# A hybrid attention and GLA decoder step: GLA's steps at thirds of a tile, and products in pairs over two PSUM banks

## Chip, core and metric

The kernel runs on one core of one Trainium2 chip. The metric is the device time of one execution in microseconds (us); the median of three runs of the kernel before is 1816.8 us (1815.72 to 1818.68). A difference of under 0.2% is taken as no change.

## What is computed

One layer of a decoder on 2048 prompt tokens and 8 x 8 sample tokens (2112 rows in all, 1024 channels). An input projection feeds two branches: windowed attention with sinks and a relative bias, and GLA, a linear attention with a decaying state. Both are gated, projected, merged, projected again by `w_o`, and normalized. Cut to what the change touches:

```python
z = jnp.einsum('btd,dn->btn', x, w_in)          # q k v g_att gq gk gv g_gla g_lr r_att r_gla
log_a = jax.nn.log_sigmoid(g_lr @ w_gk_up + b_gk) / 16
# GLA, per head and chunk; b is the running sum of log_a in the chunk
qt, kt, kend = qc * exp(b), kc * exp(-b), kc * exp(b_last - b)
o = qt @ S + where(causal, qt @ kt.T, 0) @ vc
S = exp(b_last) * S + kend.T @ vc
o_gla = o * rsqrt(mean(o * o, -1) + EPS) * gla_norm_w
h_att = (o_att * silu(g_att)) @ w_pa
h_gla = (o_gla * silu(g_gla)) @ w_pg
merged = sigmoid(r_att) * h_att + sigmoid(r_gla) * h_gla
x = layer_norm(DN_ALPHA * x + merged @ w_o, ln_g, ln_b)
```

## The kernel before

**Products.** Nearly all of TensorE's (PE's) time goes into float32r products of a 128 x 128 piece of weights with 352 columns of x. A factor is split into a high and a low part, so that each 128-row step takes three products: high x high, high weights x low x, low weights x high x (lines 1297 to 1299). A *group* is one product of blocks: 4 steps, 12 matmuls (6 in the sets a0 to a2), summed in one PSUM bank. The list `groups` holds 719 of them in program order, in nine sets: x0, x1, a0, u0, x2, a1, u1, a2, u2. The x sets (input projection and the two merge gates) use Strassen's scheme with seven products, numbered 1, 7, 6, 4, 5, 2, 3 in order of issue, and two column blocks (j = 0, 1) run side by side: product 1 of j = 0, product 1 of j = 1, product 7 of j = 0, and so on. Both take the same x and different weights. The four banks pd_74 to pd_77 serve in turn: products 1, 6, 5, 3 of one j share a bank, 7, 4, 2 another. The a and u sets (`w_pa`, `w_pg`) use eight plain block products; there two neighbours have the same weights and different x.

**The loop over groups** does the following for each `g`: it starts the weight loads of group g+9 (`w_first`) and of kept weights for g+5, splits the weights of group g+4 (`w_make`: POOL adds blocks at line 339, ACT casts at line 142, DVE subtracts at line 143; six buffers `wp`), issues the 12 matmuls, calls `combine`, which takes the result out of its bank (ACT copies at lines 375 and 379 for products 1, 7, 6; DVE adds at 384, 390, 396 for 4, 5, 2; a sink such as ACT's line 186, 199 or 211 for product 3), and then lets side work run: `xdo` makes the next set's x, and `tick` runs what `at(t, ...)` put down for this tick. A tick is four steps, about one group. PE follows this order exactly; the other engines' instructions are ordered by a scheduler.

**Side work on PE** is plain float32 and uses a pool `pa` of four more banks, handed out in turn. For GLA each head has tiles of 128 tokens, `st` ticks apart (5.0, 5.8 and 6.3 in the three GLA phases). A tile has four steps:
- v (`gla_v`, lines 1052 and 1053): three transposes; ACT's line 1054 copies them out (`gv`).
- a (`gla_a`, line 1062): scores; DVE's line 1064 masks them out (`aper`).
- b (`gla_b`, lines 1084, 1086, 1087): output and state, two banks, called op and sp here. DVE's line 1092 takes sp into the state `S`; ACT's 1071, POOL's 1072 and 1073 and ACT's 1074 take op through the norm (`on`).
- c (`gla_c`, line 1101): transposes of `on`; DVE's line 1103 multiplies them into `sg`.

With u the tile's number, v and a stand at u, b at u + 3/2, c at u + 3. So one tick holds c (of tile u-3), v and a together, and the tick half a tile later holds b. Each tile takes five banks of the four: c, v, a, op, sp; so sp gets the bank that c had half a tile earlier, and a the bank that op had.

**Gates.** `gate` (lines 699 to 719) takes four banks at once for one half of a set: four matmuls (704), eight activations out of them (708, 709), four Exp (713), four Ln (715, under another activation table), four DVE steps and stores. It runs twice per x set.

Of the kernel before, what the change touches and what calls it, by code (L numbers as in the profile page):

```python
# [15 lines left out]
AF = mybir.ActivationFunctionType  # L16
ALU = mybir.AluOpType
# [4 lines left out]
P = 128  # L22
# [4 lines left out]
NS = NB * TS  # L27
# [9 lines left out]
GH = 4  # L37
# [20 lines left out]
def kernel(ctx, tc, io):  # L58
    nc = tc.nc
    mm = nc.tensor.matmul  # L60
# [35 lines left out]
    def mt(tag, n, bufs, dt=F32, name=None):  # L96
        return M["p"].tile([P, n], dt, tag=tag, name=name or tag, bufs=bufs)
# [26 lines left out]
    def at(t, fn):  # L124
        side.setdefault(max(int(t), now[0]), []).append(fn)
# [383 lines left out]
    ops = {}  # L509
# [16 lines left out]
    def lowrank(o):  # L526

        s = o.s
        ps = pa()
        for k in range(4):  # L530
            for j in range(4):
                r = slice(32 * j, 32 * j + 32)
                mm(ps[r, :T], wg[:, k + 4 * (j // 2), :], o.r[j // 2, j % 2][:, k * T:(k + 1) * T], start=(k == 0),
                   stop=(k == 3), tile_position=(0, 32 * j))
        g_ = mtile("fin", name="glh")
        nc.scalar.copy(g_, ps[:, :T])
        for j in range(4):
            r0 = 16 * (j // 2)
            nc.gpsimd.dma_start(gl_d[r0:r0 + 16, toks(s, j % 2)], g_[32 * j:32 * j + 16])
# [39 lines left out]
        o0.mix(r0[0, 1], r0[0, 1], r0[0, 0], ALU.subtract)  # L579
        o0.make(5, r0[0, 1])  # L580

    for g, f in ((4, lambda: o0.make(3, r0[1, 1])), (6, c7), (10, c6), (12, c4), (14, lambda: lowrank(o0)), (14, c5)):
# [116 lines left out]
    def gate(B):  # L699
        ts = toks(B["s"], B["t"])  # L700
        ps = [pa() for _ in range(GH)]
        for h in range(GH):
            r = slice(32 * h, 32 * h + 32)
            mm(ps[h][:, :T], wgk[r], B["x"][r], start=True, stop=True, tile_position=(32 * h, 0))
        zs, ms = [], []
        for h in range(GH):
            z, m = mtile("fin", name="zg"), mt("lg", T, 4, name="mg")
            nc.scalar.activation(z, ps[h][:, :T], AF.Abs, bias=bgk[:, h:h + 1])
            nc.scalar.activation(m, ps[h][:, :T], AF.Relu, scale=-1.0, bias=nbgk[:, h:h + 1])
            zs.append(z)  # L710
            ms.append(m)
        for z in zs:
            nc.scalar.activation(z, z, AF.Exp, scale=-1.0)
        for z in zs:
            nc.scalar.activation(z, z, AF.Ln, bias=1.0)
        for h in range(GH):
            nc.vector.scalar_tensor_tensor(ms[h], ms[h], -1.0, zs[h], ALU.mult, ALU.subtract)
            nc.sync.dma_start(zg_d[h][:, ts], ms[h])
            wrote(zg_d[h], 0, ts)

    AS = {}
# [433 lines left out]
    def gla_phase(s, t0, t1):  # L1155
        at(t0, lambda: mpool(f"cg{s}"))
        at(t0, rings)
        nu = sum(-(-T_ // P) for _, T_ in GCH[s]) * GH
        b0 = t0 + 14
        st = (t1 - b0 - 3) / (nu + 2)  # L1160
        u = 0
        for h, (c0, T_) in ([(h, c) for c in GCH[s] for h in range(GH)] if s == 1 else
                            [(h, c) for h in range(GH) for c in GCH[s]]):
            if True:
                last = c0 + T_ == NT
                Tp = T_ - (NS if last else 0)
                nt = Tp // P
                B = dict(h=h, t0=c0, T=T_, Tp=Tp, nt=nt, last=last)
                tt = lambda v: b0 + st * v + 0.01
                b = tt(u)  # L1170
                at(b - 13, lambda B=B: gla_load(B))
                at(b - 10, lambda B=B: gla_load_v(B))
                at(b - 8, lambda B=B: gla_z(B))
                at(b - 3, lambda B=B: gla_kq(B))
                for i in range(nt):
                    at(tt(u + i), lambda B=B, i=i: gla_v(B, i))
                    at(tt(u + i), lambda B=B, i=i: gla_a(B, i))
                    at(tt(u + i + 3 / 2), lambda B=B, i=i: gla_b(B, i))
                    at(tt(u + i + 3), lambda B=B, i=i: gla_c(B, i, P, i * P))
                at(tt(u + 1) + 3, lambda B=B: gla_load_g(B))  # L1180
                o = tt(u + nt)
                u += nt
                if last:
                    u += 1
# [4 lines left out]
                    at(o + 6, lambda B=B: samp_b(B, 0))  # L1189
                    at(o + 8, lambda B=B: samp_b(B, 2))  # L1190
                    at(o + 11, lambda B=B: gla_c(B, "s", NS, B["Tp"]))
                    at(o + 12, lambda B=B: gla_store(B))
                else:
                    at(tt(u + 2) + 1, lambda B=B: gla_store(B))

    for s in range(MS):
        lo_ = {}
        for t in range(2):
            B = dict(s=s, t=t)
            g0 = base[XS[s]] + (17 if s == 0 else 2)  # L1200
            at(g0 + 4 * t, lambda B=B: gate_load(B))
            at(g0 + 5 + 4 * t, lambda B=B: gate(B))
    e = att_phase(0, 32)
    for s in range(MS):
        t1 = base[XS[s + 1]] + 30 if s < MS - 1 else base[U2] - 3
# [61 lines left out]
    half = 0  # L1267
    nm, nq = 8, 0
    NG = len(groups)
    for g, (n, q, i, s, p, b, ch) in enumerate(groups):  # L1270
        if 8 <= g + LR < NG:
            w_first(g + LR)
        if g + LK < NG:
            w_kept(g + LK)
        while nm < NG and nm <= g + (LM + 1 if groups[nm][3] == 0 and seq[groups[nm][0]] == "x0" else LM):
            w_make(nm)
            nm += 1
        for f in late.pop(g, ()):
            with tc.issue_after(pin["r"].ins):
                f()  # L1280
        while nq < NG and nq <= g + (LP + 4 if groups[nq][1] is PA_ else LP):
            _, q_, i_, s_, p_, _, _ = groups[nq]
            parts[nq] = q_.partners(i_, p_, s_)
            nq += 1
        xh, xl = ops[n].op[i[1:] if type(i) is tuple else i]
        w = wps.pop(g)
        m = q.kh * P
        if g == 8:
            banks2 = [pa() for _ in range(4)]
        ps = (banks[b] if b < 4 else banks2[b - 4])[:, :T]  # L1290
        if n == U2 and g >= start_of[U2] + 16:
            ps = banks2[b][:, :T]
        for k in range(q.kh):
            ks, ts = slice(k * P, (k + 1) * P), slice(k * T, (k + 1) * T)
            first = k == 0 and not (ch and i in (6, 4, 5, 3)) and not (type(i) is tuple and i[1])
            wh, wl = w[:, ks], w[:, m + k * P:m + (k + 1) * P]
            mm(ps, wh, xh[:, ts], start=first, stop=False, skip_group_check=ch)  # L1297
            mm(ps, wh, xl[:, ts], start=False, stop=False, skip_group_check=ch)  # L1298
            mm(ps, wl, xh[:, ts], start=False, stop=(k == q.kh - 1 and not (type(i) is tuple and i[1] == 0)), skip_group_check=ch)  # L1299
        combine(g, ps)  # L1300
        for f in xdo.get(g, ()):
            f()
        half += q.kh
        while half >= 4:
            half -= 4
            tick()
        if n == U2:
            d = g - start_of[U2]
            if d == 15:
                banks2 = [pa() for _ in range(4)]  # L1310
            if d in (4, 8, 12, 16):
                wo.append(wo_load(len(wo)))
            if d >= 28 and len(wo) < 7:
                wo.append(wo_load(len(wo)))
            if d == 3:
                ox = M["p"]
                xf, x, xr0 = load_m(1, 0, TM), [], []
            if d >= 5 and xf:
                x += [part(xf.pop(0))]
    assert not any(side.values()), [k for k in side if side[k]]  # L1320
    right.close()
    sb = right.enter_context(tc.tile_pool(name="ob", bufs=1, side="right", reuse_waits="tile"))
# [232 lines left out]
```

## Time and profile before

| | |
|---|---|
| median of three runs | 1816.8 us |
| profiled execution: its own time | 1816.59 us |
| its span, first to last instruction | 1814.8 us |
| PE, weight loads, DVE, ACT, POOL busy | 97%, 91%, 58%, 46%, 18% |
| mean granted clock | 0.994 |
| DMA | 452 MB, 249 GB/s |
| sets x0, x1, a0, u0 start at | 4.5, 446.8, 861.7, 900.4 us |
| sets x2, a1, u1, a2, u2 start at | 974.4, 1399.7, 1439.8, 1522.9, 1560.5 us |

In the timeline a row gives start, length, engine, line, what is written from what, and in brackets the idle time of the engine ahead of it with what ended it. Matmul rows overlap, so the distance of two starts, not the length, is what a matmul costs. In the view of waits a row reads: who waited, for whom, us in total, how often, the longest. In the view of windows each engine has its busy time and (x) its instructions, then PE's granted clock.

### The profile page before, as it was taken

Reading aid. Unit: us, or ns where it says so; the run is one execution under the profiler, and the core shown is the slowest. Engines: PE = TensorE matmul, PEld = TensorE weight load, DVE = VectorE, ACT = ScalarE, POOL = GpSimd, SP = SyncE. Lnnn points to the kernel's source line nnn. Section 1 sums busy time; section 2 is a strip of 40 time slices with the busy share of each in tenths; the row PEclk is TensorE's granted clock in tenths of the full one; section 3 lists DMA queues with packets and bytes.
Section 4 is the critical chain, followed back from the end, with each engine's and each line's share of the span. In section 5 each row is a group of like instructions: output and inputs, shape, how many; then the busy total and the mean of one; then the engine's idle time right before and its main releaser. Section 6 shows DMA issues by size and latency. Waiting matters only on the chain.

```text
span 1814.8 us, 31047 instructions
## 1 busy us (share of the span) xinstructions
PE 1768.1 (97%) x10850; PEld 1654.2 (91%) x10850; DVE 1059.9 (58%) x2077; ACT 837.0 (46%) x1983; POOL 334.0 (18%) x473
## 2 busy tenths in 40 slices
PE   8999999998999999999999999999999999999997
PEld 7898998998998899999999998899999889998886
DVE  7577677667546654445666456554455744536665
ACT  5856555555836553545435646444445422310100
POOL 5334344644100000000033000000000022021111
PEclk9999999999999999999999999999999999999999
DMA  6799588887698779878976897688879977975531
GB/s 211 253 313 322 208 315 283 306 274 238 223 302 275 227 244 302 275 251 276 318 217 145 276 306 223 219 293 299 284 266 320 301 197 200 325 174 175 171 102 53
DMA packets 291052, 452.03 MB, mean 249 GB/s; under 512 B 29693, under 2 KB 210229, under 8 KB 290880
## 3 DMA queue, kind: packets, MB, share of 16 engines
q1 hardware_dynamic: 263536, 416.27, 69.3%
q10 hardware_dynamic: 19536, 24.47, 3.8%
q0 software_dynamic: 7824, 9.31, 3.6%
q8 instruction: 86, 1.41, 0.3%
q14 instruction: 70, 0.57, 0.1%
HBM read 297.52 MB, written 153.30 MB: 248 GB/s over the span
## 4 chain that ended last, share of the span: by engine, by line
PE 71%; DMA 11%; ACT 4%; DVE 4%; issue 4%; POOL 3%; SPq 1%; ACTq 0%; DVEq 0%; POOLq 0%
PE pd L1297 17%; PE pd L1299 16%; PE pd L1298 16%; PE pd L1361 3%; PE pd L1360 3%; PE pd L1362 3%; POOL ws L339 2%; DMA part<-ra_d 2%; DMA ws<-w_g 1%; DMA r<-ug_d 1%; PE pa L812 1%; DMA mg_d<-fin 1%; PE pa L798 1%; PE pa L1086 1%; PE pa L766 1%
## 5 line engine op out<-in xcount | busy, mean ns | idle before, releaser
L143 DVE TENSOR_TENSOR wp<-ws,wp 128x512 fp32r<-128x512 f32 (+1 forms) x396 | 270.1, 687 | 214.6 <-ACT wp L142 195.5
L142 ACT CAST wp<-ws 128x512 fp32r<-128x512 f32 (+1 forms) x396 | 232.8, 594 | 202.0 <-PE pd L1299 137.8
L339 POOL TENSOR_TENSOR ws<-ws 128x256 f32<-128x256 f32 x162 | 141.5, 908 | 157.0 <-DVE wp L143 93.7
L1072 POOL TENSOR_SCALAR sq<-sq 128x1 f32<-128x1 f32 x68 | 21.4, 314 | 731.9 <-ACT on L1071 731.9
L375 ACT COPY m<-pd 128x352 f32<-128x352 f32 x146 | 65.4, 452 | 84.8 <-PE pd L1299 83.6
L1297 PE MATMUL pd<-x7h,wp 128*128 128x352 f32 x292 | 98.0, 336 | 5.2 <-ACT fin L186 4.3
L1361 PE MATMUL pd<-woh,x 128*128 128x512 f32 x256 | 100.0, 391 | 0.0
L1360 PE MATMUL pd<-woh,x 128*128 128x512 f32 x256 | 99.8, 390 | 0.0
L1362 PE MATMUL pd<-wol,x 128*128 128x512 f32 x256 | 99.5, 389 | 0.0
L1297 PE MATMUL pd<-x2h,wp 128*128 128x352 f32 x292 | 97.9, 335 | 0.0
L1297 PE MATMUL pd<-x3h,wp 128*128 128x352 f32 x292 | 97.8, 335 | 0.0
L1297 PE MATMUL pd<-x1h,wp 128*128 128x352 f32 x292 | 97.1, 333 | 0.7 <-ACT fin L186 0.7
L1297 PE MATMUL pd<-x6h,wp 128*128 128x352 f32 x292 | 97.3, 333 | 0.0
L1297 PE MATMUL pd<-x4h,wp 128*128 128x352 f32 x292 | 96.9, 332 | 0.0
L1297 PE MATMUL pd<-x5h,wp 128*128 128x352 f32 x292 | 96.3, 330 | 0.0
L1299 PE MATMUL pd<-x7h,wp 128*128 128x352 f32 x292 | 94.8, 325 | 1.1 <-DVE wp L143 1.1
L1299 PE MATMUL pd<-x5h,wp 128*128 128x352 f32 x292 | 94.9, 325 | 0.0
L1298 PE MATMUL pd<-x5l,wp 128*128 128x352 f32 x292 | 94.8, 325 | 0.0
L1298 PE MATMUL pd<-x1l,wp 128*128 128x352 f32 x292 | 94.8, 325 | 0.0
L1299 PE MATMUL pd<-x1h,wp 128*128 128x352 f32 x292 | 94.8, 325 | 0.0
L1299 PE MATMUL pd<-x3h,wp 128*128 128x352 f32 x292 | 94.8, 325 | 0.0
L1298 PE MATMUL pd<-x3l,wp 128*128 128x352 f32 x292 | 94.7, 324 | 0.0
(441 smaller groups left out, 5252.4 us busy)
## 6 DMA issues: line engine op xcount, KB each, us to landing
wp<-wk_w_g SPq DMA_DIRECT2D x96, 512.0 KB
ws<-w_g SPq DMA_DIRECT2D x120, 256.0 KB
wk_w_g<-wp SPq DMA_DIRECT2D x48, 512.0 KB
wp<-wk_w_ra SPq DMA_DIRECT2D x32, 512.0 KB
wp<-wk_w_rg SPq DMA_DIRECT2D x32, 512.0 KB
ws<-w_at SPq DMA_DIRECT2D x54, 256.0 KB
wp<-wk_w_at SPq DMA_DIRECT2D x24, 512.0 KB
ws<-w_pg SPq DMA_DIRECT2D x48, 256.0 KB
```

Of the source, the lines that this page charges most:

```text
L142: pin["a"] = nc.scalar.copy(dst_h, src)
L143: i = eng.tensor_tensor(dst_l, src, dst_h.bitcast(F32), ALU.subtract)
L339: nc.gpsimd.tensor_tensor(o[:, c], x[:, c], y[:, c], op)
L375: nc.scalar.copy(A[i], ps)
L766: mm(ps[kv][:, j, k0:], A["zq"][r, g0 + j, :], A["kk"][r, 0, k0:], start=True, stop=True, tile_position=(kv * HD, 0))
L1072: nc.gpsimd.tensor_scalar(sq[:n], sq[:n], EPS, None, op0=ALU.add)
L1297: mm(ps, wh, xh[:, ts], start=first, stop=False, skip_group_check=ch)
L1298: mm(ps, wh, xl[:, ts], start=False, stop=False, skip_group_check=ch)
L1299: mm(ps, wl, xh[:, ts], start=False, stop=(k == q.kh - 1 and not (type(i) is tuple and i[1] == 0)), skip_group_check=ch)
L1360: mm(ps, xh[:, xs], hi, start=(k == 0), stop=False)
L1361: mm(ps, xl[:, xs], hi, start=False, stop=False)
L1362: mm(ps, xh[:, xs], lo, start=False, stop=(k == KT - 1))
```

## The change

Three things change, and no instruction is added or removed but a few activation table loads.

1. GLA's steps: v and a stay at u, b moves to u + 5/3, c to u + 10/3. A tile's distance is now `(t1 - b0 - 3) / (nu + 7/3)`, some 1.5% less. The sample tile's steps and the store of a head move with them.
2. The gate runs in two halves of two banks, one tick apart (in x1 and x2), with the Exp and Ln part two ticks after the second half; the second gate of x1 and x2 comes 7 ticks after the first and not 4. The low-rank product of x0 moves behind group 15.
3. Groups run in pairs. If the next group has the same x (or the same weights, in the a and u sets) and another bank, both are issued together, matmul by matmul in turn; side work of the first group's tick runs in the middle of the pair, after the first half of its steps; `combine` of both follows behind the pair, then the second tick's side work. 349 pairs and 21 single groups come out. Weight making for the second group of a pair is still called for after the pair before.

```diff
-                    at(tt(u + i + 3 / 2), lambda B=B, i=i: gla_b(B, i))
-                    at(tt(u + i + 3), lambda B=B, i=i: gla_c(B, i, P, i * P))
+                    at(tt(u + i + 5 / 3), lambda B=B, i=i: gla_b(B, i))
+                    at(tt(u + i + 10 / 3), lambda B=B, i=i: gla_c(B, i, P, i * P))
...
+            at(g0, lambda B=B: gate(B, 0))
+            at(g0 + (s > 0), lambda B=B: gate(B, 2))
+            at(g0 + 3 * (s > 0), lambda B=B: gate_end(B))
...
+    def together(g):
+        if g + 1 == NG:
+            return False
+        (n, q, i, s, p, b, ch), (n_, q_, i_, s_, p_, b_, ch_) = groups[g:g + 2]
+        if n != n_ or b == b_ or type(i) is not type(i_):
+            return False
+        if i == i_:
+            return (q, p) != (q_, p_)
+        return type(i) is tuple and i[:2] == i_[:2] and (q, p) == (q_, p_)
...
+        for k in range(half * h, half * h + h):
+            ks, kl, ts = slice(k * P, (k + 1) * P), slice(m + k * P, m + (k + 1) * P), slice(k * T, (k + 1) * T)
+            for ps, w, (xh, xl) in a:
+                mm(ps, w[:, ks], xh[:, ts], start=open_ and k == 0, stop=False, skip_group_check=ch)
+            for ps, w, (xh, xl) in a:
+                mm(ps, w[:, ks], xl[:, ts], start=False, stop=False, skip_group_check=ch)
+            for ps, w, (xh, xl) in a:
+                mm(ps, w[:, kl], xh[:, ts], start=False, stop=close and k == q.kh - 1, skip_group_check=ch)
...
+    for g, (n, q, i, s, p, b, ch) in enumerate(groups):
+        before(g)
+        if g == 8:
+            banks2 = [pa() for _ in range(4)]
+        if g not in got:
+            gs = [g, g + 1] if together(g) else [g]
+            got.update(zip(gs, products(gs, 0)))
+            if len(gs) == 2:
+                aside(g, n, q)
+            products(gs, 1)
+            for h in gs:
+                combine(h, got[h])
+        if g == gs[-1]:
+            aside(g, n, q)
```

On PE, in x0's product 2 of two column blocks (pd_74 and pd_75 are banks, x2h and x2l the two parts of x, wp the weights), the order was one bank after the other:

```order
L1297 MATMUL pd0_74<-x2h_164,wp_1146 128x352
L1298 MATMUL pd0_74<-x2l_165,wp_1146 128x352
L1299 MATMUL pd0_74<-x2h_164,wp_1146 128x352
...
L1297 MATMUL pd1_75<-x2h_164,wp_1166 128x352
L1298 MATMUL pd1_75<-x2l_165,wp_1166 128x352
L1299 MATMUL pd1_75<-x2h_164,wp_1166 128x352
```

Now, at the same place on PE, the two go in turn:

```order
L1317 MATMUL pd0_74<-x2h_164,wp_1160 128x352
L1317 MATMUL pd1_75<-x2h_164,wp_1166 128x352
L1319 MATMUL pd0_74<-x2l_165,wp_1160 128x352
L1319 MATMUL pd1_75<-x2l_165,wp_1166 128x352
L1321 MATMUL pd0_74<-x2h_164,wp_1160 128x352
L1321 MATMUL pd1_75<-x2h_164,wp_1166 128x352
```

The bank and the weights change with every matmul, x only with every second; both banks are done at the end of the pair.

On ACT, in x1 (a column pair of GLA's keys, m the copies of products 1 and 7, u of product 6), a copy out of a bank and a cast of new weights took turns:

```order
L375 COPY m_7764<-pd_77 128x352
L142 CAST wp<-ws 128x512
L375 COPY m_7780<-pd_74 128x352
...
L375 COPY m_7808<-pd_75 128x352
L142 CAST wp<-ws 128x512
...
L375 COPY m_7831<-pd_76 128x352
```

Now ACT has the same products' copies two by two:

```order
L375 COPY m_7776<-pd_77 128x352
L375 COPY m_7778<-pd_74 128x352
L142 CAST wp<-ws 128x512
...
L375 COPY m_7824<-pd_75 128x352
L375 COPY m_7826<-pd_76 128x352
L142 CAST wp<-ws 128x512
```

A bank is used again two groups (24 matmuls) after its pair ends, where it was three groups (36) after its group.

On PE, one GLA tile of the first phase (pa the side banks) stood in two places, c, v and a, then b:

```order
L1101 MATMUL pa<-ident,on 128x128 x2
L1052 MATMUL pa<-ident,zvv 128x128 x2
L1053 MATMUL pa<-ident,ek 128x128
L1062 MATMUL pa<-dm,em 128x128
...
L1084 MATMUL pa<-S_217,gb 128x256
L1086 MATMUL pa<-gv 128x256
L1087 MATMUL pa<-gv,aper_206 128x256
...
L1101 MATMUL pa<-ident,on 128x128 x2
```

Between a and b lie 24 of the main matmuls, between b and the next c 36. The same tile's PE rows now:

```order
L1053 MATMUL pa<-ident,zvv 128x128 x2
L1054 MATMUL pa<-ident,ek 128x128
L1063 MATMUL pa<-dm,em 128x128
...
L1102 MATMUL pa<-ident,on 128x128 x2
...
L1085 MATMUL pa<-S_217,gb 128x256
L1087 MATMUL pa<-gv 128x256
L1088 MATMUL pa<-gv,aper_206 128x256
...
L1053 MATMUL pa<-ident,zvv 128x128 x2
```

Here 24 main matmuls lie between a and c, 12 between c and b, 24 between b and the next v. The banks follow as v, a, c, op, sp, so that sp gets v's bank (36 matmuls later here), c gets op's (48 here, 36 at the least), and a gets c's (36 here, 48 in most tiles).

More of the change, by code (lines that the diff above doesn't have):

```diff
@@ L580, in c5 @@
         o0.make(5, r0[0, 1])
-    for g, f in ((4, lambda: o0.make(3, r0[1, 1])), (6, c7), (10, c6), (12, c4), (14, lambda: lowrank(o0)), (14, c5)):
+    for g, f in ((4, lambda: o0.make(3, r0[1, 1])), (6, c7), (10, c6), (12, c4), (15, lambda: lowrank(o0)), (15, c5)):
         xdo.setdefault(g, []).append(f)
@@ L697, in gate_load, with gate, gate_end @@
             nc.sync.dma_start(x[32 * h:32 * h + 32], gl_d[:, toks(B["s"], B["t"])])
-    def gate(B):
+    def gate(B, h0):
+        ps = [pa() for _ in range(2)]
+        for j in range(2):
+            r = slice(32 * (h0 + j), 32 * (h0 + j) + 32)
+            mm(ps[j][:, :T], wgk[r], B["x"][r], start=True, stop=True, tile_position=(32 * (h0 + j), 0))
+        for j in range(2):
+            h = h0 + j
+            z, m = B["z", h], B["m", h] = mtile("fin", name="zg"), mt("lg", T, 4, name="mg")
+            nc.scalar.activation(z, ps[j][:, :T], AF.Abs, bias=bgk[:, h:h + 1])
+            nc.scalar.activation(m, ps[j][:, :T], AF.Relu, scale=-1.0, bias=nbgk[:, h:h + 1])
+    def gate_end(B):
         ts = toks(B["s"], B["t"])
-        ps = [pa() for _ in range(GH)]
         for h in range(GH):
-            r = slice(32 * h, 32 * h + 32)
-            mm(ps[h][:, :T], wgk[r], B["x"][r], start=True, stop=True, tile_position=(32 * h, 0))
-        zs, ms = [], []
+            nc.scalar.activation(B["z", h], B["z", h], AF.Exp, scale=-1.0)
         for h in range(GH):
[L707 to L715, printed above, removed]
+            nc.scalar.activation(B["z", h], B["z", h], AF.Ln, bias=1.0)
         for h in range(GH):
-            nc.vector.scalar_tensor_tensor(ms[h], ms[h], -1.0, zs[h], ALU.mult, ALU.subtract)
-            nc.sync.dma_start(zg_d[h][:, ts], ms[h])
+            m = B["m", h]
+            nc.vector.scalar_tensor_tensor(m, m, -1.0, B["z", h], ALU.mult, ALU.subtract)
+            nc.sync.dma_start(zg_d[h][:, ts], m)
             wrote(zg_d[h], 0, ts)
@@ L1159, in gla_phase @@
         b0 = t0 + 14
[L1160 removed]
+        st = (t1 - b0 - 3) / (nu + 7 / 3)
         u = 0
@@ L1188, in gla_phase @@
                     at(tt(u - 1 + 0.5) + 2, lambda B=B: nc.sync.dma_start(io["o_sp"][B["h"]], S_t[sstate[B["h"]]]))
[L1189 to L1192, printed above, removed]
+                    o = max(o + 6, tt(u - 1 + 4 / 3) + 1)
+                    at(o, lambda B=B: samp_b(B, 0))
+                    at(o + 2, lambda B=B: samp_b(B, 2))
+                    at(o + 5, lambda B=B: gla_c(B, "s", NS, B["Tp"]))
+                    at(max(o + 6, tt(u + 4 / 3) + 1), lambda B=B: gla_store(B))
                 else:
-                    at(tt(u + 2) + 1, lambda B=B: gla_store(B))
+                    at(tt(u + 7 / 3) + 1, lambda B=B: gla_store(B))
     for s in range(MS):
-        lo_ = {}
         for t in range(2):
             B = dict(s=s, t=t)
-            g0 = base[XS[s]] + (17 if s == 0 else 2)
-            at(g0 + 4 * t, lambda B=B: gate_load(B))
-            at(g0 + 5 + 4 * t, lambda B=B: gate(B))
+            g0 = base[XS[s]] + (22 + 4 * t if s == 0 else 7 + 7 * t)
+            at(g0 - 5, lambda B=B: gate_load(B))
+            at(g0, lambda B=B: gate(B, 0))
+            at(g0 + (s > 0), lambda B=B: gate(B, 2))
+            at(g0 + 3 * (s > 0), lambda B=B: gate_end(B))
     e = att_phase(0, 32)
@@ L1269, with before @@
     NG = len(groups)
-    for g, (n, q, i, s, p, b, ch) in enumerate(groups):
+    def before(g):
+        nonlocal nm, nq
         if 8 <= g + LR < NG:
@@ L1284 @@
             nq += 1
[L1285 to L1290, printed above, removed]
-        if n == U2 and g >= start_of[U2] + 16:
[L1292 to L1299, printed above, removed]
@@ L1300, with bank @@
-        combine(g, ps)
+    def bank(g):
+        n, q, i, s, p, b, ch = groups[g]
+        if n == U2 and g >= start_of[U2] + 16:
+            return banks2[b][:, :T]
+        return (banks[b] if b < 4 else banks2[b - 4])[:, :T]
+    def together(g):
[7 more added lines that the diff above has]
+        return type(i) is tuple and i[:2] == i_[:2] and (q, p) == (q_, p_)
@@ new lines, in products @@
+    def products(gs, half):
+        a = []
+        for g in gs:
+            n, q, i, s, p, b, ch = groups[g]
+            a.append((bank(g), wps.pop(g) if half else wps[g], ops[n].op[i[1:] if type(i) is tuple else i]))
+        open_ = not (ch and i in (6, 4, 5, 3)) and not (type(i) is tuple and i[1])
+        close = not (type(i) is tuple and i[1] == 0)
+        m, h = q.kh * P, q.kh // 2
+        for k in range(half * h, half * h + h):
[6 more added lines that the diff above has]
+                mm(ps, w[:, kl], xh[:, ts], start=False, stop=close and k == q.kh - 1, skip_group_check=ch)
+        return [ps for ps, _, _ in a]
@@ L1301, with aside @@
+    def aside(g, n, q):
+        nonlocal half, ox, xf, x, banks2
         for f in xdo.get(g, ()):
```

2 lines of the change are left out of this document (added).

## Prediction

> **What bounds the kernel now.** I read the page's busy times first, then PE's waits, then the stretches where its clock fell, then the timeline around the longest waits. PE's line of the page:
>
> ```profile
> PE 1768.1 (97%) x10850; PEld 1654.2 (91%) x10850; DVE 1059.9 (58%) x2077; ACT 837.0 (46%) x1983; POOL 334.0 (18%) x473
> ```
>
> PE is busy 97% of the span, so the kernel gets shorter only if PE's products come closer together or its idle time goes. The waits that the change touches (who waited, for whom, us in total, times, longest):
>
> ```profile
> PE pa L1086 <- DVE sg L1103: 4.6, 3, 3.6
> PE pa L1086 <- ACT gv L1054: 3.7, 2, 3.4
> PE pa L1086 <- ACT on L1074: 3.1, 1, 3.1
> PE pd L1297 <- DVE fin L219: 2.4, 3, 1.2
> PE pa L1062 <- ACT on L1074: 2.3, 1, 2.3
> ...
> PE pa L1062 <- DVE S L1092: 1.2, 1, 1.2
> PE pa L1101 <- ACT mg L709: 1.2, 1, 1.2
> ```
>
> The rows with pa are GLA's and the gates' banks: 4.6 + 3.7 + 3.1 + 2.3 + 1.2 + 1.2 = 16.1 us, which parts 1 and 2 of the change address. The row with pd is of main banks not yet taken out, which part 3 can make worse. Behind four of these waits (at 307, 430, 440 and 1481) the clock falls; the first and the last of the four, and the stretch that follows the first (columns: window, length, then each engine's busy time with its instructions, PE's clock, DMA share, GB/s):
>
> ```profile
> 307.32:310.73 3.41, 3.41 (x13) 3.32 (x12) 3.41 (x9) 2.86 (x7) 0.00 (x0) 0.50 0.95 339
> 1481.51:1484.92 3.41, 3.41 (x12) 3.15 (x11) 2.98 (x6) 1.42 (x5) 1.91 (x3) 0.50 0.34 61
> 311.00:314.41 3.41, 3.41 (x23) 3.41 (x23) 1.10 (x3) 2.21 (x5) 0.91 (x2) 1.00 0.96 304
> ```
>
> At clock 0.50 PE issues 12 or 13 matmuls where it issues 23 at 1.00: 10 x 3.41 / 23 = 1.5 us lost in each window, beside the wait itself.
>
> **Part 1, GLA's steps.** The longest `sg` wait, in the timeline:
>
> ```profile
> 303.22 0.52 SPq L1008 DMA_DIRECT2D sg<-z_gg  x1
> ...
> 306.07 0.41 DVE L1103 TENSOR_TENSOR sg<-pa,sg 128x256 f32<-128x256 f32 x1
> ...
> 306.54 0.70 PE L1086 MATMUL pa<-gv 128*128 128x256 f32 x2 [3.60 <-DVE sg L1103]
> ```
>
> Step b's sp bank was c's bank, and c's reader (DVE, 306.07) sat behind a load begun at 303.22. Now sp gets v's bank, 36 matmuls after v, and c's bank goes to the next a, 36 to 48 matmuls later instead of 24. A main matmul costs 0.160 us (rows in part 3), so twelve of them are 1.92 us. c's reader has 1.9 to 3.8 us more, which covers 3.6 and both shorter ones: 4.6 goes. The rows behind the longest wait for `gv` and, last, behind that for `on` before step a:
>
> ```profile
> 420.91 0.27 PE L1053 MATMUL pa<-ident,ek 128*128 128x128 f32 x1
> ...
> 428.52 0.47 ACT L1054 COPY gv<-pa 128x384 f32<-128x384 f32 x1
> ...
> 439.81 0.47 ACT L1074 ACTIVATE on<-pa,sq 128x256 f32<-128x256 f32 x1 [1.73 <-POOL sq L1073]
> ```
>
> ACT's copy came 7.6 us after the transposes. b stands 36 matmuls behind v now, not 24: 1.92 us more, so of 3.4 stay 1.5 and the 0.3 goes. `on` before b's second product (3.1): op's bank serves c next, 48 matmuls later instead of 36, so 1.2 stay. `on` before a (2.3, at 440): the phase's last tiles, where ACT itself waited for POOL; I leave it whole. `S` before a (1.2): the bank it held goes to a v that is no farther or one group farther, so half, 0.6. The gate's row (1.2): halves of two banks a tick apart leave 0.3. Left: 1.5 + 1.2 + 2.3 + 0.6 + 0.3 = 5.9 of 16.1, a gain of **10.2 us** (0, if the lateness just moves on, to 16.1).
>
> Windows of low clock: the one at 307 follows a wait that goes; of the other three (430, 440 and 1481, behind 3.4, 2.3 and 3.1 us) two waits shrink to 1.5 or less, and whether 1.5 us still drops the clock no row decides. I count two windows: **-3.0** (0 to -6.0).
>
> **Part 3, PE's rate.** Two products in turn would be faster if a change of bank, or the same x twice, let the next matmul start sooner. The program before has such bank changes at each group's end. There are 464 where neither side work nor a wait comes between. Their distance of starts has a mean of 0.1600 us, against 0.1612 over 7,159 distances inside a bank. The first of them, then the last:
>
> ```profile
> 11.72 0.32 PE L1299 MATMUL pd<-x1h,w 128*128 128x352 f32 x1
> 11.88 0.32 PE L1297 MATMUL pd<-x1h,w 128*128 128x352 f32 x1
> ```
>
> ```profile
> 1591.18 0.32 PE L1299 MATMUL pd<-x(1, 1)h,wp 128*128 128x352 f32 x1
> 1591.35 0.32 PE L1297 MATMUL pa<-x(0, 0)h,wp 128*128 128x352 f32 x1
> ```
>
> The means differ by 1.3 ns; with some 7,400 new bank changes (11 of 12 of 8052) that bounds the gain at 9.4 us. Consecutive distances in these rows scatter by 10 ns, which is more, and the first of these pairs has a common x1h at no gain: I take **0** (-9.4 to +3).
>
> **Part 3, the banks' cover.** A bank had three groups, 5.8 us, to be taken out, now two, 3.9. The first of a pair ends 1.9 us later than before, the second is needed 1.9 us earlier. An example in x2, where a gate's activations hold ACT until 1016 (the first row ends the group, the last is its bank's next use):
>
> ```profile
> 1011.47 0.32 PE L1299 MATMUL pd<-x3h,wp 128*128 128x352 f32 x1
> ...
> 1018.16 0.44 ACT L186 COPY fin<-pd 128x352 f32<-128x352 f32 x1
> ...
> 1018.66 0.19 PEld L1297 LDWEIGHTS pd<-x7h,wp 128*128 128x128 f32 x1 [0.28 <-ACT fin L186]
> ```
>
> The group that ended at 1011.8 is out at 1018.6, just when its bank is used again. In a pair that bank is the second's, and due 1.93 us sooner: a new wait of nearly 1.9. So I shifted the due time of each second bank over the whole trace: 39 of 599 hand-overs fall behind, in 17 places from 76 to 1576 us; the worst lateness of each place, summed, is 12.1 us. Of these, 2.6 sit at gates that part 2 splits, and about half of the others where late loads hold PE anyway. I take **+6** (0 to +12.1). The Trainium skill says in "Perfetto Trace Analysis", Optimizing Tensor Performance, Matmuls, that groups should rotate through banks so that one's evacuation overlaps the next one's matmuls; that speaks against closing two banks at once. By that rule alone the whole 12.1 would be due; the trace agrees only at those 17 places, since elsewhere DVE (58%) and ACT (46%) are done in time.
>
> **Part 3, weights.** The second of a pair needs its weights right after the pair's first matmul, one group earlier, while they are made at the old place:
>
> ```profile
> 8.46 0.69 DVE L143 TENSOR_TENSOR w<-ws,w 128x512 fp32r<-128x512 f32 x1 [0.31 <-ACT w L142]
> ...
> 9.61 0.49 PE L1297 MATMUL pd<-x1h,w 128*128 128x352 f32 x1
> ```
>
> Group 1's were done at 9.15 and used at 9.61; a group earlier is 7.7, so PE waits 1.5 there, though less has then to be caught up. Of 161 second products whose weights are made, six lie under zero. **+2** (0 to +5).
>
> **The gates' table loads.** ACT's order has 17 table loads now for 13; the gate's row (times, us in total, ns of one):
>
> ```profile
> L715 ACT ACT_TABLE_LOAD x6 | 7.7, 1283 | 0.1
> ```
>
> Four more are 5.1 us of ACT's. Only what stands behind them when a bank is due costs PE: **+1** (0 to +5). Nothing else is added; PE's side work interrupts the pairs as often as the groups before.
>
> **Sum.** The profiled execution took 1816.59 us (the span and 1.8 around it), 0.2 from the median of 1816.8, so no correction. 1816.6 - 10.2 - 3.0 + 0 + 6 + 2 + 1 = **1812.4 us**. A measurement of this kernel tells about 0.2%, 3.6 us, from no change.
>
> **The rivals.** *Slower: the banks' cover decides.* ACT and DVE take banks out in order behind casts and gates, both banks of a pair ask at once, and PE waits wherever a bank is taken out over 3.9 us behind the pair's end. That is 12.1 us at the 17 places, 5 for weights, 2 for table loads, and the new waits make half of GLA's gain void (-6.6): 1816.6 + 12.1 + 5 + 2 - 6.6 = 1829. For it speaks the row at 1018.16, against it that 560 of 599 hand-overs have the time. It decides once the sum of new pd waits passes 13.2 us.
>
> *No change: the lateness is fixed in time.* Many of PE's waits end on something that a load released:
>
> ```profile
> 1478.43 0.78 ACT L142 CAST x(0, 1)h<-r 128x704 fp32r<-128x704 f32 x1 [11.68 <-DMA r<-ug_d]
> ```
>
> ACT waited 11.7 us for this load, and `on` (the 3.1 us wait) stood behind it in ACT's order. One more group of distance then moves PE's wait to the next consumer. GLA's gain shrinks to the `sg` row and its window, 4.6 + 1.5 = 6.1, and the banks' 6 takes it back: 1816.6 - 6.1 + 6 = 1816.5.
>
> *Much faster: turns shorten a matmul.* The eight rows of 512 columns from which I take a matmul's fixed part begin and end so:
>
> ```profile
> 1679.80 0.39 PE L1362 MATMUL pd<-wol,x 128*128 128x512 f32 x1
> ...
> 1681.38 0.39 PE L1360 MATMUL pd<-woh,x 128*128 128x512 f32 x1
> ```
>
> Seven distances in 1.58 us make 0.226 each, 66 ns more than 0.160 for 160 more columns, or 0.41 ns a column; 352 columns are then 145 ns, and 15 are fixed. If they were a wait on the bank, turns would hide them: 15 ns x 8052 = 121 us, 1691. The 464 bank changes speak against it. The Trainium skill gives 352 / 2.4 + 2.5 = 149 ns for a warm matmul ("TensorE: Matmul & The Clock Gate", Back-to-back issue gap); an estimate by it would be 11 ns x 8052 = 89 us and 1728. Traces here never show it.
>
> **How the numbers follow.** The forecast has 0.48: 0.41 of it faster, 0.07 within 0.2% (the sum with a bound or two at its dear end). No change has 0.20, 0.17 of it within, 0.01 faster, 0.02 slower; the slower rival 0.29, of which 0.27 slower, 0.02 within; turns 0.03. So faster 0.45, same 0.26, slower 0.29. The range's low end has GLA's waits and two windows gone at no price, 1816.6 - 16.1 - 3.0 = 1797.5, about 1797; its high end is the slower rival with the full 5 of the table loads, 3 more than its 2: 1832. It leaves out the turns and the tails.
>
> **What would show it.** Right: PE's rows for `sg` gone and `gv`'s under 2; no half clock at 307; matmul starts still 0.160 apart within a pair; new rows L1317 <- fin (L186, L201, L219, L227) and <- u, of some 6 us together, behind gates and in the a and u sets; a wait of about 1.5 near 8 us. The slower rival shows pd waits of 13 us and more over before's; no change shows pa waits of 10 us and more under other names. Starts under 0.155 apart would make the prediction wrong at its base, and so would starts over 0.162, as that alone costs 16 us.

## The result, and the profile after

The changed kernel takes 1851.3 us (median of five runs, 1844.5 to 1854.1) against 1818.0 for the kernel before (1815.7 to 1821.0): 1.0167 times as long by the estimate from all runs, 95% interval 1.0149 to 1.0185 (the two medians alone give 1.0183). By the medians it is slower by 33 us, where 1812.4 was forecast and 1832 was the end of the range. The profiled execution has a span of 1849.9 us, 35.1 more than before.

PE's line of the page, to be held against the one of before:

```profile
PE 1782.9 (96%) x10850; PEld 1660.7 (90%) x10850; DVE 1048.5 (57%) x2077; ACT 830.7 (45%) x1987; POOL 335.7 (18%) x473
```

As many matmuls, 14.8 us more of PE's busy time and 20.3 us more of its idle time. The idle time, in PE's waits (us in total, times, longest):

```profile
PE pd L1317 <- DVE fin L219: 7.2, 3, 3.0
PE pa L753 <- ACT pT L803: 6.3, 2, 4.9
PE pa L1102 <- ACT on L1075: 6.0, 1, 6.0
PE pd L1317 <- ACT fin L186: 5.2, 3, 4.6
PE pd L1317 <- ACT x1h L142: 4.6, 1, 4.6
PE pd L1317 <- ACT w L142: 4.3, 1, 4.3
PE pd L1317 <- DVE fin L201: 3.9, 2, 2.3
PE pd L1317 <- DVE fin L390: 3.2, 2, 2.7
PE pd L1317 <- DVE fin L227: 2.9, 1, 2.9
PE pd L1317 <- DMA wp<-wk_w_g: 2.9, 4, 1.1
PE pd L1317 <- DVE u L392: 2.7, 1, 2.7
PE pd L1317 <- DMA wp<-wk_w_ra: 2.4, 2, 1.8
```

Of the rows of before at GLA's banks, those for `sg`, `gv` and `S` are gone, and the two for `on` (3.1 and 2.3) have become a single wait of 6.0. In their place stand waits at the main banks (fin, u) and for weights (w, wp), and one kind that no one looked for: attention's transposes (L753) wait 6.3 us for ACT's copy `pT`.

Next, the windows of half clock. There are eight before PE's last stretch where there were five. Shown are the first, the fourth and the fifth (window, length, each engine's busy time with its instructions, PE's clock, DMA share, GB/s):

```profile
87.97:94.79 6.82, 5.21 (x18) 4.89 (x18) 4.29 (x7) 3.10 (x7) 0.90 (x1) 0.50 0.69 252
...
456.61:463.43 6.82, 5.97 (x21) 5.97 (x22) 6.26 (x13) 4.86 (x13) 3.65 (x5) 0.50 0.67 224
719.43:722.84 3.41, 3.41 (x14) 3.41 (x13) 0.00 (x0) 0.00 (x0) 0.00 (x0) 0.50 0.76 286
```

Together they last 34.1 us, before 17.1. The Trainium skill describes a case like this under "TensorE: Matmul & The Clock Gate", A second HAM failure mode: psum-queue depth-cycling: PE goes idle for short times between groups of matmuls and its clock swings between half and full. The trace agrees where PE waited: each of these windows comes with one wait of 2.2 to 6.0 us, or with two of 1.1 and 0.9 us close together. It doesn't follow at once from the length, as waits of 2.3 us (at 123) and 2.7 us (at 417) left the clock at 1.00. No stretch of this trace without a wait dropped its clock, however often the banks changed.

Last, the pace inside a pair (a row here holds two matmuls, one for each bank):

```profile
620.04 0.48 PE L1317 MATMUL pd<-x6h,wp 128*128 128x352 f32 x2
620.36 0.48 PE L1319 MATMUL pd<-x6l,wp 128*128 128x352 f32 x2
620.68 0.48 PE L1321 MATMUL pd<-x6h,wp 128*128 128x352 f32 x2
```

0.32 us from row to row, 0.160 for a matmul, as before. Turns neither shorten nor lengthen a product.

**Where the 35 us are.** Grouped from the same view of both traces: waits at main banks 10.2 before, 28.0 now (+17.8); for weights and the first x 5.9, 14.8 (+8.9); GLA and gates 16.8, 6.4 (-10.4); attention's copies 1.3, 6.8 (+5.5); half clock outside the waits, from matmul distances over 0.16 in these windows, +7.5. The sixth item is none of the five:

```profile
600.64 0.32 PE L1299 MATMUL pd<-x6h,wp 128*128 128x352 f32 x1
600.89 1.94 PE L812 MATMUL pa<-pT,vt 128*64 128x512 f32 x8
602.76 0.43 PE L1297 MATMUL pd<-x4h,wp 128*128 128x352 f32 x1
603.03 0.32 PE L1298 MATMUL pd<-x4l,wp 128*128 128x352 f32 x1
```

These are rows of before. After side work the first distance between main matmuls is 0.27 us here (0.25 to 0.35 at most places) and not 0.16. PE comes back from side work 221 times before and 280 times now, since GLA's c has its own place in a tile. That adds 5.8 us behind side work and 1.1 us ahead of it, while the distances inside side work are 3.9 us shorter: +3.0 in all.

Two smaller items remain. Distances between main matmuls at full clock add 5.4 us: 43 of them are over 0.2 us where 16 were, as some waits are too short to be listed in the view of waits, and as the first distance behind a wait is longer, too. The stretch at the program's start is 1.1 us shorter outside its waits. With the wait at L533 (1.9 before, 0.4 now) the sum comes to the 35.1.

### The profile page after: what moved, and what is told of

Read it like the earlier page. It is cut to its first block, busy times and chain, and to the rows that moved or that the text cites. A ratio compares the mean times of both kernels' runs of the same rounds, so it can differ in the third digit from the quotient of the medians.

```text
span 1849.9 us, 31078 instructions
## 1 busy us (share of the span) xinstructions
PE 1782.9 (96%) x10850; PEld 1660.7 (90%) x10850; DVE 1048.5 (57%) x2077; ACT 830.7 (45%) x1987; POOL 335.7 (18%) x473
## 4 chain that ended last, share of the span: by engine, by line
PE 72%; DMA 8%; ACT 5%; issue 5%; DVE 4%; POOL 4%; SPq 2%; ACTq 0%; DVEq 0%; POOLq 0%
PE pd L1317 17%; PE pd L1319 16%; PE pd L1321 16%; PE pd L1403 3%; PE pd L1402 3%; PE pd L1404 3%; POOL ws L339 2%; DMA wp<-wk_w_g 1%; PE pa L767 1%; PE pa L799 1%; PE pa L813 1%; PE pa L1088 1%; PE pa L1087 1%; PE pa L1085 1%; DMA part<-ra_d 1%
## 5 line engine op out<-in xcount | busy, mean ns | idle before, releaser
L1317 PE MATMUL pd<-x7h,wp 128*128 128x352 f32 x292 | 77.9, 342 | 9.6 <-ACT fin L186 4.6
L780 ACT ACTIVATE s<-s,nm 128x256 f32<-128x256 f32 (+1 forms) x128 | 62.4, 489 | 41.5 <-DVE nm L777 41.5
L1317 PE MATMUL pd<-x3h,wp 128*128 128x352 f32 x292 | 76.6, 339 | 3.8 <-DVE fin L390 3.2
L1317 PE MATMUL pd<-x1h,wp 128*128 128x352 f32 x292 | 76.4, 337 | 3.3 <-DVE u L392 2.7
L1317 PE MATMUL pd<-x5h,wp 128*128 128x352 f32 x292 | 75.7, 335 | 3.7 <-DMA wp<-wk_w_ra 1.8
L142 ACT CAST x<-xst 128x384 fp32r<-128x384 f32 (+2 forms) x48 | 22.9, 487 | 122.1 <-PE pd L1403 115.8
L1317 PE MATMUL pd<-x4h,wp 128*128 128x352 f32 x292 | 75.3, 335 | 0.0
L1321 PE MATMUL pd<-x7h,wp 128*128 128x352 f32 x292 | 72.6, 326 | 0.6 <-DVE wp L143 0.6
L1075 ACT ACTIVATE on<-pa,sq 128x256 f32<-128x256 f32 x68 | 32.2, 473 | 90.4 <-POOL sq L1074 90.4
L1321 PE MATMUL pd<-x3h,wp 128*128 128x352 f32 x292 | 72.4, 326 | 0.0
L1319 PE MATMUL pd<-x7l,wp 128*128 128x352 f32 x292 | 72.2, 325 | 0.0
L1319 PE MATMUL pd<-x3l,wp 128*128 128x352 f32 x292 | 72.2, 325 | 0.0
```

The lines of the kernel that those rows point to most:

```text
L142: pin["a"] = nc.scalar.copy(dst_h, src)
L780: nc.scalar.activation(sl, sl, AF.Exp, bias=nm[:, h:h + 1], accum_out=sm[:, h:h + 1])
L1075: nc.scalar.mul(on[:n], o, sq[:n])
L1317: mm(ps, w[:, ks], xh[:, ts], start=open_ and k == 0, stop=False, skip_group_check=ch)
L1319: mm(ps, w[:, ks], xl[:, ts], start=False, stop=False, skip_group_check=ch)
L1321: mm(ps, w[:, kl], xh[:, ts], start=False, stop=close and k == q.kh - 1, skip_group_check=ch)
```

## The experiments

Theory A: the pairs cost it, since banks and weights are due sooner and come free later. Theory B: GLA's moved steps cost it. Later letters split A. Each line gives the ratio to the kernel before on the same chip, with its 95% interval; 1% is 18 us. Each edit is against the changed kernel where nothing else is said.

| run | us | ratio | interval |
|---|---|---|---|
| e1, GLA and gate, no pairs | 1813.4 | 0.9980 | 0.9968 to 0.9993 |
| e2, pairs alone | 1864.7 | 1.0263 | 1.0243 to 1.0284 |
| e3, pairs, one product after the other | 1817.0 | 1.0001 | 0.9986 to 1.0015 |
| e4, weights called for earlier | 1854.4 | 1.0203 | 1.0179 to 1.0226 |
| e5, second's first matmul ahead | 1840.8 | 1.0119 | 1.0094 to 1.0144 |
| e6, first's last matmul behind | 1835.2 | 1.0089 | 1.0061 to 1.0118 |
| e7, both | 1850.8 | 1.0172 | 1.0145 to 1.0200 |
| e8, seven weight buffers | 1830.5 | 1.0058 | 1.0035 to 1.0081 |
| e9, only the second's bank early | 1845.2 | 1.0154 | 1.0131 to 1.0177 |
| e10, only its weights early | 1833.7 | 1.0091 | 1.0070 to 1.0112 |
| e16, control of e9 and e10 | 1832.6 | 1.0077 | 1.0064 to 1.0090 |
| e13, only the first's bank late | 1863.3 | 1.0248 | 1.0228 to 1.0267 |
| e14, only its weights late | 1859.5 | 1.0227 | 1.0208 to 1.0247 |
| e15, control of e13 and e14 | 1844.1 | 1.0136 | 1.0121 to 1.0152 |
| e11, gate alone | 1817.6 | 1.0004 | 0.9989 to 1.0018 |
| e12, e1 with seven weight buffers | 1818.7 | 1.0008 | 0.9991 to 1.0025 |

**e1 and e2: the change in two halves.** Each has one half of the change on top of the kernel before.

> GLA's steps at thirds and the gate in halves, products one after the other as before. Theory A (the pairs cost it: banks have 3.9 us and not 5.8 to be taken out, and second weights are due a group earlier): without pairs only GLA's and the gate's own effects are left: the 16 us of waits at the side banks shrink by some 10, and some 7 come back since PE leaves the main products 118 times more, each return costing 0.107 us in the trace of after; 1810 to 1818 us. Theory B (the moved GLA steps cost it: returns, and new waits of 12 us for on and pT): 1830 us or more.

> Pairs alone; GLA's steps at halves and the gate whole, as before. Theory A: nearly the whole loss is here, 1843 to 1855 us, with pd waits of 40 us against 16 before. Theory B: 1818 to 1828 us.

Theory B falls: GLA's steps and the gate alone gain 0.2%. Pairs alone cost 2.6%, more than the whole change; with pairs GLA's steps and the gate save 13 us by the medians or 17 by the ratios, without them 4. The 118 returns in e1's expectation should be 59: PE comes back 280 times in e1's trace, too, and 221 times before. e1's waits at the side banks:

```profile
PE pa L1102 <- ACT on L1075: 3.8, 1, 3.8
...
PE pa L1102 <- DVE S L1093: 3.2, 1, 3.2
PE pa L1063 <- DVE sg L1104: 2.8, 1, 2.8
```

`sg`, `S` and `on` still make PE wait, but at c and a (L1102, L1063) where b waited before: 9.8 us in three waits. All waits at GLA's and the gate's banks come to 10.8 us in e1 and 16.8 before. The rival "the lateness is fixed in time" was half right here.

**e3: what in a pair costs it.**

```diff
-        for k in range(half * h, half * h + h):
+        todo = [(k, p) for p in a for k in range(q.kh)]      # a pair's first product, then its second
+        todo = todo[half * q.kh:(half + 1) * q.kh]
```

> The changed kernel, but the two products of a pair stand one after the other (12 matmuls into one bank, the first tick's side work, 12 into the other); both banks are still taken out behind the pair, so the first is taken out a group later than before and the second as before. Second weights are due where they were before. Theory A1 (cover of the banks): 1838 to 1850 us, near the changed kernel. Theory A2 (alternation itself, by the second weights due a group earlier, or by a matmul that costs more when bank and weights change each time): most of the loss goes, 1815 to 1825 us. Matmul starts stay 0.160 to 0.161 us apart in both.

All 33 us go, though `combine` of both still stands behind the pair. So the loss hangs on turns. The place of `combine` and of the side work costs some 4 us, if anything (e3 against e1, whose intervals overlap).

**e4: weights called for a group earlier.** `before(g + 1)` moves ahead of the pair.

> The changed kernel, but what each group calls for ahead (weight loads, making of weights, loads of partial sums) is called for both groups of a pair ahead of the pair, so weights are made a group earlier in the order. Theory A2 by weights: 6 to 14 us of the loss come back, 1836 to 1844 us, and the waits of PE for wp and its loads go. Theory A1: no gain or a loss of a few us, since two casts now stand ahead of the banks in ACT's order: 1848 to 1860 us.

No gain. Weights are not late for want of an earlier place in the order. ACT's casts of weights show why (times, busy us, mean ns, then the idle time just before them and what ended most of it); the changed kernel, then e4:

```profile
L142 ACT CAST wp<-ws 128x512 fp32r<-128x512 f32 (+1 forms) x396 | 230.6, 598 | 261.0 <-PE pd L1321 179.8
```

```profile
L142 ACT CAST wp<-ws 128x512 fp32r<-128x512 f32 (+1 forms) x396 | 231.6, 595 | 332.8 <-PE pd L1321 268.1
```

Casts wait for PE to give a buffer back, and the earlier they stand, the longer ACT waits there (268 us, not 180) with banks' copies behind it.

**e5 to e7: due times without turns.** A pair's 24 matmuls in blocks, with only two or three changes of bank (K is a product's list of matmuls, 0 the pair's first product, 1 its second):

```diff
+e5  todo = [(1, K[0])] + [(0, e) for e in K] + [(1, e) for e in K[1:]]
+e6  todo = [(0, e) for e in K[:-1]] + [(1, e) for e in K] + [(0, K[-1])]
+e7  todo = [(1, K[0])] + [(0, e) for e in K[:-1]] + [(1, e) for e in K[1:]] + [(0, K[-1])]
```

> The changed kernel, but of a pair PE issues one matmul of the second product, the twelve of the first, then the other eleven of the second. The second's bank and weights are due at the pair's start, as in turn; the first's weights are released after thirteen matmuls, as one after the other. Theory D (due times of the second cost it): near the changed kernel, 1840 to 1855 us. Theory C (the first's weights are held to the pair's end, a buffer comes free a group later, and ACT's cast that waits for it holds ACT's and DVE's other work): near the kernel with one after the other, 1815 to 1825 us. Theory M (it needs a change of bank and weights at each matmul): 1815 to 1825 us as well.

> The changed kernel, but of a pair PE issues eleven matmuls of the first product, the twelve of the second, then the last of the first. The first's weights are held to the pair's end, as in turn; the second's bank and weights are due one matmul earlier than one after the other. Theory D: 1815 to 1825 us. Theory C: near the changed kernel, 1838 to 1855 us. Theory M: 1815 to 1825 us.

> The changed kernel, but one matmul of the second product, eleven of the first, eleven of the second, one of the first: the due times and the release of the changed kernel with four changes of bank in a pair and not 24. Theories D and C: 1845 to 1856 us, the changed kernel's time. Theory M: 1815 to 1825 us. In turn itself is then innocent or not.

e7 takes as long as the changed kernel (1.0172 and 1.0167) with three changes of bank in a pair in place of 23. Changing bank and weights at each matmul is innocent; the whole loss lies in when the second begins and when the first ends. Each end alone costs too (e5 1.2%, e6 0.9%), so D and C both hold.

**e8 and e12: a seventh buffer for weights.** In the pools `wp` goes from 6 to 7, `fin` from 10 to 8; e12 does the same to e1.

> The changed kernel with seven buffers for split weights and not six; the room comes from the buffers for results (fin), eight and not ten. Theory C: 8 us or more come back, 1825 to 1843 us, and ACT's casts wait less for PE. Theory D by banks: 1848 us and up, since banks have no more time and results have fewer buffers.

> GLA's steps at thirds and the gate in halves, no pairs, with seven buffers for split weights and eight for results (fin). If the seventh buffer helps only where pairs hold the weights longer (theory C with Dw), 1810 to 1818 us, no faster than with six (1813). If weights are short everywhere, 1800 to 1808 us, and the gain of seven buffers in the changed kernel says little of pairs.

With pairs the buffer brings back 20 us of 33, without them it brings nothing (1.0008, where six gave 0.9980). The casts' row in e8, then in e6, where only the first's end is late:

```profile
L142 ACT CAST wp<-ws 128x512 fp32r<-128x512 f32 (+1 forms) x396 | 228.7, 597 | 186.3 <-PE pd L1321 126.4
```

```profile
L142 ACT CAST wp<-ws 128x512 fp32r<-128x512 f32 (+1 forms) x396 | 230.6, 594 | 356.6 <-PE pd L1323 283.2
```

The seventh buffer leaves PE's waits at the main banks as they are (28.0 us, as in the changed kernel). What goes is attention's wait for `pT` (6.3 to 0.4), 4.7 us of the waits for weights, and half of the half clock (34.1 to 17.1 us). ACT's idle time at casts is not by itself a measure of the loss: it is larger in e6 (283), which loses 0.9%, than in the changed kernel (180), which loses 1.7%.

**e9, e10 and e16: at the pair's start, bank or weights?** On top of e3, one matmul of 32 columns ahead of a pair, overwritten by the product that follows:

```diff
+            mm(a[B][0][:, :32], a[W][1][:, :P], a[0][2][0][:, :32], start=True, stop=True, skip_group_check=True)
+            # e9: B=1, W=0 (second's bank, first's weights); e10: B=0, W=1; e16: B=0, W=0
```

> The kernel with the two products one after the other, and ahead of a pair one small matmul (32 columns, overwritten later) with the first's weights into the second's bank: the second's bank is due at the pair's start, its weights are not. The small matmul costs the same in this kernel and the next, 345 of them at 0.03 to 0.16 us, 10 to 55 us over the 1817 without it, so the two are compared with each other. Theory Db (the second's bank is what is due too early): 10 to 20 us more than the next. Theory Dw (its weights): 10 to 20 us less.

> The same, but the small matmul takes the second's weights and writes into the first's bank: the second's weights are due at the pair's start, its bank is not. Theory Db: 10 to 20 us less than the kernel with the bank early. Theory Dw: 10 to 20 us more.

> The control of the two early kernels: ahead of the pair the same small matmul (156 of them in the trace), with the first's weights into the first's bank, so nothing of the second is due early. By the price in the traces, 5 us: 1820 to 1824 us, so that the second's bank due early costs some 23 us and its weights some 11. If the small matmul itself costs more: 1830 us or above, and the bank's part is 15 us or less.

There are 157 small matmuls and not 345, as the other pairs add to a bank that is not opened anew and were left alone. They cost 0.76% by themselves (e16 against e3), 0.09 us each, three times what was expected. Against that control the bank due early costs 0.77%, 14 us, and the weights due early 0.14%, less than the intervals tell. PE's largest waits at the main banks in e9, then in e10:

```profile
PE pd L1315 <- ACT fin L186: 5.8, 3, 2.0
PE pd L1315 <- DVE fin L201: 5.5, 1, 5.5
...
PE pd L1315 <- ACT fin L199: 4.0, 4, 1.4
```

```profile
PE pd L1315 <- ACT fin L186: 3.8, 1, 3.8
...
PE pd L1315 <- DVE fin L201: 0.7, 2, 0.4
```

e9's L199, 4.0 us, has no row in e10. All waits at the main banks come to 21.0 us in e9 and 7.3 in e10.

**e13, e14 and e15: at the pair's end, bank or weights?** On top of e3, behind each of the 349 pairs a matmul of 32 columns with zeros, added to a bank:

```diff
+            mm(a[B][0][:, :32], a[W][1][:, :P], zr, start=False, stop=close, skip_group_check=True)
+            # e13: B=0, W=1 (first's bank, second's weights); e14: B=1, W=0; e15: B=1, W=1
```

> The kernel with the two products one after the other, and behind each of the 349 pairs a small matmul of the second's weights with zeros (32 columns) added to the first's bank: the first's bank cannot be taken out before the pair's end, its weights are released where they were. The small matmul costs some 0.03 us (188 ns for it and its neighbour, against 160, in the two kernels before), 10 us in all, so about 1827 us with no other effect; again the two kernels are compared with each other. Theory Cw (the first's weights held to the pair's end cost the 18 us of that part): 1827 to 1832 us, and 8 to 18 us less than the next. Theory Cb (the first's bank, taken out a group later): 1838 to 1848 us, 8 to 18 us more than the next.

> The same with the first's weights, zeros, and the second's bank: the first's weights are held to the pair's end, its bank is free to be taken out after its own twelve matmuls. Theory Cw: 1838 to 1848 us. Theory Cb: 1827 to 1832 us.

> The control of the two late kernels: behind each pair the same small matmul, but with the second's weights into the second's bank, so neither the first's bank nor its weights are held. The traces of the two put the price of 349 small matmuls at 22 to 27 us of PE. If both holdings cost what is above that: 1838 to 1844 us, some 20 us under the two late kernels. If the small matmul itself makes the loss (for instance as it holds the second's bank): 1855 to 1865 us.

Against the control, the first's bank held to the pair's end costs 1.12%, 20 us, and its weights held cost 0.91%, 17 us. Both times lie above what was expected, as 349 small matmuls cost 25 us and not 10. Neither theory holds by itself: each holding is enough. They don't add up, since e6 has both and costs 0.9%. The casts' row in e14, then in the control:

```profile
L142 ACT CAST wp<-ws 128x512 fp32r<-128x512 f32 (+1 forms) x396 | 231.3, 593 | 299.3 <-PE pd L1323 221.2
```

```profile
L142 ACT CAST wp<-ws 128x512 fp32r<-128x512 f32 (+1 forms) x396 | 232.9, 595 | 202.4 <-PE pd L1323 88.2 <-PE pd L1321 50.5 <-POOL ws L339 25.5
```

Holding the weights alone makes ACT stand 221 us in all at casts until PE is done, against 139 (88.2 behind the small matmul, 50.5 behind a product's last).

The two holdings make PE wait at different places. The bank held makes it wait at the main banks: 25.8 us in e13, 15.5 in the control, 8.3 in e14. The weights held make it wait at the side banks: for GLA 17.8 us in e14, 9.1 in the control, 4.5 in e13; and for attention's `pT`, of which the control has no row (e14, then e13):

```profile
PE pa L753 <- ACT pT L803: 7.7, 2, 4.3
```

```profile
PE pa L753 <- ACT pT L803: 1.8, 2, 1.2
```

**e11: the gate alone.** Only the gate's halves, on top of the kernel before.

> The kernel before with only the gate in halves; GLA's steps as before, no pairs. If GLA's thirds pay for their 59 more returns to the main products (0.1 us each, 6 us), this is slower than the kernel with both (1813): 1815 to 1818 us. If they do not, it is as fast or faster: 1807 to 1813 us.

No difference, so e1's gain is most likely GLA's thirds, which pay for their 59 returns (the intervals of e1 and e11 just overlap). e1 is the fastest kernel here, 0.2% under the one before; the nearest with turns is e8, at 0.6% over.

## Why the prediction was wrong

The sign was wrong, and the measured time lies beyond even the slower rival. By steps:

- **PE's rate, 0: right.** 0.160 us in a pair, and e7 has the loss without turns.
- **GLA's steps, -10.2: right in number, by luck.** The waits fell by 10.4 us in the trace of the changed kernel, but PE waited 27 us more for main banks and weights there, which probably gave the engines behind GLA's steps time. Without pairs they fell by 6.0 (e1, 16.8 to 10.8), and the kernel gained 4. "PE's side work interrupts the pairs as often as the groups before" was false as well. It rests on the order of before; in the order of after c stands by itself, which is 59 returns more, 3.0 us net.
- **The clock, -3.0: wrong sign, +7.5.** New waits opened windows faster than GLA's closed them; the one meant to go, at 307, came back at 320 behind a wait for `u` (2.65 us).
- **The banks' cover, +6 with 12.1 as its end: this step failed.** The due time of each second bank was shifted with ACT's and DVE's times left as they were. The measured +17.8 is beyond that end. The step said itself that the first's bank ends 1.9 us later, and then priced only the second's; holding the first's bank costs 20 us alone (e13 against e15).
- **Weights, +2 (0 to 5): this step failed, too.** It asked only when the second's weights are needed. Even that was mis-sized where it was read: the wait of 1.5 us near 8 came as 4.3 us at 9.5. A group was taken as 1.92 us there, but PE's first matmuls start 0.29 us apart and more, and in the kernel before group 1 began 5.1 us behind group 0. Most of it was caught up (2.9 us behind after 24 matmuls, 1.0 after 300), and in the 157 pairs that e10 tests early weights cost next to nothing. The step did not ask when the first's buffer is given back: after 24 matmuls and not 12. That costs 17 us alone (e14 against e15), and a seventh buffer undoes most of the loss (e8).
- **Table loads, +1:** no wait in the trace hangs on them; not tried by themselves.
- **A slip outside the sum:** for turns that shorten a matmul, 1691 was taken from the forecast (1812.4 - 121) and 1728 from the kernel before (1816.6 - 89). From the kernel before the first is 1695.6. Nothing hangs on it.

How weights held too long reach a place that has nothing to do with weights shows in a long new wait of the changed kernel, during attention:

```profile
177.62 0.45 ACT L379 COPY u<-pd 128x352 f32<-128x352 f32 x1 [4.12 <-PE pd L1321]
...
183.64 0.62 ACT L142 CAST wp<-ws 128x512 fp32r<-128x512 f32 x1
...
185.69 1.43 POOL L339 TENSOR_TENSOR ws<-ws 128x256 f32<-128x256 f32 x2 [29.44 <-DVE wp L143]
...
189.37 2.76 POOL L339 TENSOR_TENSOR ws<-ws 128x256 f32<-128x256 f32 x4
...
192.16 1.66 ACT L142 CAST wp<-ws 128x512 fp32r<-128x512 f32 x3 [4.37 <-POOL ws L339]
...
193.72 1.06 ACT L803 COPY pT<-pa 128x512 f32<-128x512 f32 x2
...
194.35 0.69 PE L753 MATMUL pa<-ident,kk 128*128 128x128 f32 x2 [4.86 <-ACT pT L803]
```

The same place before:

```profile
166.65 0.45 ACT L379 COPY u<-pd 128x352 f32<-128x352 f32 x1 [3.08 <-PE pd L1299]
167.00 0.62 ACT L142 CAST wp<-ws 128x512 fp32r<-128x512 f32 x1
...
169.61 1.43 POOL L339 TENSOR_TENSOR ws<-ws 128x256 f32<-128x256 f32 x2 [19.99 <-DVE nm L776]
...
178.07 1.66 ACT L142 CAST wp<-ws 128x512 fp32r<-128x512 f32 x3 [1.46 <-POOL ws L339]
...
179.64 1.06 ACT L802 COPY pT<-pa 128x512 f32<-128x512 f32 x2
```

Before, a cast followed the copy `u` at once, ahead of attention's activations. Now it comes six microseconds after the copy, behind them. POOL's adds of weights, which wait here until DVE has split what was cast, begin 8.0 us ahead of `pT` where they began 10.0 us ahead, and run until 192. ACT waits 4.4 us for them at a cast (1.5 before); behind the cast stands `pT`, and PE waits 4.9 us for that. That held weights are the cause is shown by the runs: e14 has this wait (7.7 us in all), e13 hardly (1.8, as e3 with 1.6), and e8 with its seventh buffer 0.4. Loads of kept weights are caught between both ends, as their buffer is free later and needed sooner:

```profile
716.59 0.81 ACT L375 COPY m<-pd 128x352 f32<-128x352 f32 x2 [2.70 <-PE pd L1321]
...
717.79 0.40 PE L1317 MATMUL pd<-x6h,wp 128*128 128x352 f32 x1 [1.07 <-DMA wp<-wk_w_g]
...
719.05 0.40 PE L1317 MATMUL pd<-x6h,wp 128*128 128x352 f32 x1 [0.87 <-DMA wp<-wk_w_g]
```

ACT has nothing to do here (it waited 2.7 us for PE), and still PE waits twice for `wp`. Such waits are 5.3 us in the changed kernel and 4.6 in e7, which has both ends, but 0.4 in e5 and 0.2 in e6, which have one each.

Lateness is not a sum of independent places: in these rows POOL, ACT, DVE and PE pass it on. Why the two holdings don't add up is not shown by a run of its own. The traces show that PE's waits at GLA's banks shrink where those at the main banks grow (9.1 and 15.5 us in e15, 4.5 and 25.8 in e13, 4.6 and 27.7 in e6), so that one wait of PE seems to cover another; this is argued.

The slower rival had the mechanism at the banks and the sign, and priced it at 12.1 + 5. The rule that the prediction drew from the Trainium skill ("Perfetto Trace Analysis", Optimizing Tensor Performance, Matmuls: rotate banks so that taking one out overlaps the next group) was weighed as due only at 17 places. e9 and e13 agree with it: a bank due early costs 14 us, a bank ending late 20.

**Left open.** How the 22 us of e5 divide: the bank in the 157 pairs with an opened bank explains 14; the other pairs were not tried apart. And e8 changed `fin` together with `wp`; e12 against e1 suggests that this costs some 0.3% by itself, but the seventh buffer was not tried without it.

## What to carry to other kernels

Issuing two products in turn makes both hold everything for the length of both: it is one product less of cover for the second's bank, the first's bank and the first's operands. So ask of each buffer at both ends, when it is due and when it is given back, and count the ring again before the order is changed. And a shift of due times in a trace prices only the first round, and only the ends that are shifted: the lateness that it makes is handed on, as in the rows above. Here 8 us for banks and weights became 27.

## What was not expected of the hardware

A matmul of 32 columns among those of 352 starts its successor 0.03 us later, but the next distance, from that successor on, is 0.25 us and not 0.16, so that it costs some 0.115 us. Of e15's 349 some 205 stand so; the others stand right ahead of side work, which interrupts PE's stream anyway. Together they cost 1.35% (e15 against e3), 25 us or 0.07 us each. Inside PE's stream of main matmuls a change of bank and weights costs nothing; each interruption by other matmuls costs a first distance of 0.25 us or more on the way back.
